# Seven products for eight in two chunk pairs of a decoder's first FFN products, and low parts made by accumulating transfers

## The chip, the cores and the metric

One core of a Trainium2 chip runs the program. The metric is device time in microseconds (us). A core has five engines that run their own instruction lists in order: PE (TensorE, matrix products into PSUM banks), DVE (VectorE), ACT (ScalarE), POOL (GpSimd) and SP (which here only issues transfers). Instructions of different engines meet through semaphores; transfers are carried by 16 DMA engines.

## The reference

Two decoder layers over 256 tokens of width 1024. Each layer is FFN, token mixing, FFN, each followed by a layer norm. All is float32. Only the FFN matters here:

```
def swiglu(x, w_in, w_out):
    gate, up = jnp.split(x @ w_in, 2, axis=-1)      # w_in 1024 x 5632
    return (jax.nn.silu(gate) * up) @ w_out         # w_out 2816 x 1024
...
for l in range(DEPTH):                              # DEPTH = 2
    x = layer_norm(alpha * x + 0.5 * swiglu(x, ffn_w_in[l, 0], ffn_w_out[l, 0]), ...)
    x = layer_norm(alpha * x + token_mixing(x, ...), ...)
    x = layer_norm(alpha * x + 0.5 * swiglu(x, ffn_w_in[l, 1], ffn_w_out[l, 1]), ...)
```

So there are four FFNs, each with a first product (`x @ w_in`) and a second one.

## The kernel before

**Split products.** PE multiplies in a float32 form of fewer bits (`F32R`). Every operand is therefore kept as a high and a low part: ACT copies a weight tile to the high part, which rounds (L78), and DVE subtracts that from the original for the low part (L79). `split` does this, mostly in tiles of 128x1024; `stage` fetches a tile from memory through SP (L86) into one of five buffers `wst`; `stream` does both for a chunk. The parts go to six pairs of buffers `wh`, `wl` and four pairs `exh`, `exl`. `mm3` makes a product out of three matmuls: high by high (L105), high by low (L106), low by high (L107).

**First product.** The 5632 columns are cut into 11 chunks of 512 (256 gate, 256 up). A chunk has four staged tiles (8 blocks of 128 rows of the weight, two to a tile), and takes 8 blocks x 2 token tiles t x 3 = 48 matmuls of 128x512 into two PSUM banks `ph`. Chunks 0 and 1 go together, the others (single chunks) one by one; their tiles are used in order, each by 12 matmuls. Behind a chunk `act` makes `g` = silu(gate) * up with ACT (`sg`, L250) and DVE (L252). `emit_T` turns g on PE (four transposes into `ptg`, L270) and splits it; for the chunks in `FAST` it also makes sums of g's quarters (`su`) and splits them. For a single chunk it is called for the chunk before, in front of the chunk's third tile.

**Second product.** Five of the 11 chunks (`FAST`) already use seven products of quarters for eight (`fast`), with the differences of weight quarters in tiles `ts`; the others are plain.

**Order.** The engine lists are made by a scheduler of the framework when the program is built; a tile of a pool waits until its buffer's last user is done. The layer norm's gain and bias (`gb`, 1 MB) are loaded by SP while the first product runs (`load_gb`).

Of the kernel before, what the change touches and what calls it, by code (L numbers as in the profile page):

```python
# [8 lines left out]
F32 = mybir.dt.float32  # L9
# [3 lines left out]
OP = mybir.AluOpType  # L13
# [12 lines left out]
NEG = -1e30  # L26

FAST = (0, 2, 4, 6, 7)
ALPHA = float((2 * DEPTH) ** 0.25)


# [20 lines left out]
def trunk(ctx: ExitStack, tc: tile.TileContext, a: dict):  # L52
# [13 lines left out]

        return wpool.tile([P, 1024], dt, tag="ex" + side, name="ex" + side, bufs=4)

    def split(src, n, cut, more=False):

        if more:
            h, l = extra("h", F32R), extra("l", F32R)
        else:
            h = wpool.tile([P, 1024], F32R, tag="wh", name="wh", bufs=SPLIT_BUFS)
            l = wpool.tile([P, 1024], F32R, tag="wl", name="wl", bufs=SPLIT_BUFS)
        for i in range(0, n, cut):
            c = slice(i, min(i + cut, n))
            nc.scalar.activation(h[:, c], src[:, c], AF.Copy)  # L78
            nc.vector.tensor_tensor(out=l[:, c], in0=src[:, c], in1=h[:, c].bitcast(F32), op=OP.subtract)  # L79
        return h, l  # L80

    def stage(src, n, cut=1024):
# [3 lines left out]
            nc.sync.dma_start(out=t[:, c], in_=src[:, c])  # L86
        return t

    def stream(src, kcs, n, cut=1024, more=False):


        out = []
        per = 1024 // n
        for k0 in range(0, kcs, per):
            m = min(per, kcs - k0)
            st = stage(src[:, k0 * n:(k0 + m) * n], m * n, cut)
            h, l = split(st[:, :m * n], m * n, min(cut, m * n), more)
# [148 lines left out]
    def ffn(l, i, first):  # L246
        with tc.tile_pool(name="fpool", bufs=1, reuse_waits="tile") as fp:
            def act(t, ps):
                sg = fp.tile([P, 256], F32, tag="sg", name="sg", bufs=3)
                nc.scalar.activation(sg, ps[:, :256], AF.Silu)  # L250
                g = fp.tile([P, 256], F32, tag="g", name="g", bufs=3)
                nc.vector.tensor_tensor(out=g, in0=sg, in1=ps[:, 256:], op=OP.mult)  # L252
                return g

# [7 lines left out]
            def emit_T(c, gs, pt=None):  # L262

                if pt is None:
                    pt = at.tile([P, 4, P], F32, tag="sc", name="ptg", bufs=2)

                at_ = ((1, 0), (2, 3)) if c in FAST else ((0, 1), (2, 3))
                for t in range(2):
                    for k in range(2):
                        nc.tensor.transpose(pt[:, at_[k][t]], gs[t][:, k * P:(k + 1) * P], ident)  # L270
                if c not in FAST:
                    h, l = parts(pt, f"g{c}")
                    gT[c] = {(k, t): (h[:, at_[k][t]], l[:, at_[k][t]]) for k in range(2) for t in range(2)}
                    return

                a10 = fp.tile([P, P], F32, tag="a10", name="a10", bufs=2)
                nc.scalar.activation(a10, pt[:, 0], AF.Copy)
                su = fp.tile([P, 4, P], F32, tag="su", name="su", bufs=2)
# [8 lines left out]
                gT[c].update({f"s{j + 1}": (sh[:, j], sl[:, j]) for j in range(4)})  # L287

            gT = {}
            pend = None  # L290
            w = {}
            for cs in ((0, 1), *((c,) for c in range(2, NCH))):
                pss = {}
                if first and cs == (0, 1):
                    warm_up()
                    w = {0: [], 1: []}
                    for k in range(0, KC, 2):
                        for c in cs:
                            w[c] += first_blocks(a["ffin"][l, i, c], k, c == 0, c == 1)
                    load_ident()  # L300
                else:
                    for c in cs:
                        w[c] = stream(a["ffin"][l, i, c], KC, 512, 512 if c == 0 else 1024,
                                      c == (0 if i == 1 else 1))
# [8 lines left out]
                if first and cs == (4,):  # L313
                    load_consts()
                    init_consts()
                for c, t, k in order:
                    if len(cs) == 1 and (t, k) == (0, 4):

                        emit_T(*pend)
                        pend = None  # L320
                    if k == 0:
                        pss[c, t] = mm.tile([P, 512], F32, tag="mm", name="ph")
                    mm3(pss[c, t], xs(t, k), w[c][k], k == 0, k == KC - 1)
                for c in cs:
                    if pend is not None:
                        emit_T(*pend)
                    pend = (c, [act(t, pss[c, t]) for t in range(2)])
                    w.pop(c)
            gb = load_gb(l, 2 * i)


# [13 lines left out]
            def fast(c):  # L345
                b0, b1 = (stage(src[:, k * 1024:(k + 1) * 1024], 1024) for k in (2 * c, 2 * c + 1))
                lo, hi = slice(0, 512), slice(512, 1024)
                u = fp.tile([P, 1024], F32, tag="ts", name="ts", bufs=2)
                v = fp.tile([P, 1024], F32, tag="ts", name="ts", bufs=2)
                tt = nc.vector.tensor_tensor  # L350

                w00 = split(b0[:, lo], 512, 512, True)
                tt(out=u[:, lo], in0=b0[:, hi], in1=b0[:, lo], op=OP.subtract)
                tt(out=u[:, hi], in0=b1[:, hi], in1=b0[:, hi], op=OP.subtract)
                w1 = split(b1, 1024, 1024, True)
                wu = split(u, 1024, 1024, True)
                tt(out=v[:, lo], in0=b1[:, hi], in1=u[:, lo], op=OP.subtract)
                tt(out=v[:, hi], in0=b1[:, lo], in1=v[:, lo], op=OP.subtract)
                wv = split(v, 1024, 1024, True)
                for n, x, w, cols in (("p1", "a00", w00, lo), ("p2", "a01", w1, lo), ("p5", "s1", wu, lo),  # L360
                                      ("p7", "s3", wu, hi), ("p6", "s2", wv, lo), ("p3", "s4", w1, hi),
                                      ("p4", "a11", wv, hi)):
# [35 lines left out]
            for c in range(NCH - tail // 2):  # L398
# [5 lines left out]
                            for h in range(2):  # L404
                                down(t, h, k)
                if c == 0:
                    emit_T(*pend, ptl)
            last = l == DEPTH - 1 and i == 1
            for t in range(2):
                for h in range(2):  # L410
# [596 lines left out]
```

## Time and profile before

| | us |
|---|---|
| median of 3 runs (1036.57 to 1037.86) | 1037.13 |
| the profiled execution's own time | 1037.3 |
| its span, first to last instruction | 1035.3 |
| PE busy | 1018.1 |
| DVE busy | 784.8 |
| ACT busy | 551.0 |
| POOL busy | 23.3 |

Time lies 2.0 us above the span in the profiled execution. Busy is time in which an engine had at least one instruction under way; PE's is modelled, and an engine can be busy at less than its best rate.

### The profile page before, as it was taken

The page shows a single profiled execution, that of the slowest core. Times are in us where ns is not written, and L with a number is a line of the kernel's source. Part 1 is how long each engine was busy: PE and PEld are TensorE (multiplying, and loading weights), DVE is VectorE, ACT ScalarE, POOL GpSimd, SP SyncE. Part 2 cuts the span into 40 slices and gives each one's busy share as a digit, 9 for nine tenths or more (in the row PEclk, how much of TensorE's full clock was granted, in tenths as well). Part 3 has the DMA queues.
Part 4 walks back from the last instruction along what each step waited for, and adds up shares of the span by engine and source line. Part 5 has one row for each costly group of instructions (what it writes and reads, how often), then busy time and mean ns, then how long its engine had stood idle before and what let it go on. Part 6 is the DMA issues. An engine that isn't in the chain of part 4 may idle for free.

```text
span 1035.3 us, 14159 instructions
## 1 busy us (share of the span) xinstructions
PE 1018.1 (98%) x5166; PEld 830.0 (80%) x5166; DVE 784.8 (76%) x1313; ACT 551.0 (53%) x916; POOL 23.3 (2%) x35
## 2 busy tenths in 40 slices
PE   9999999999999999999999999999999999999997
PEld 6888878878877888888878888888888778888785
DVE  6765978975989566687986668898679885657877
ACT  7554546435785445553644456544358744446451
POOL 0000000100000000000000000002000000000000
PEclk9999999999999999999999999999999999999998
DMA  9866646753463466674585656559515544666641
GB/s 341 295 204 185 214 148 191 263 189 114 133 230 85 165 189 182 174 232 143 171 283 163 184 183 207 178 156 326 185 34 176 187 136 152 185 190 189 197 150 41
DMA packets 59541, 190.22 MB, mean 184 GB/s; under 512 B 7120, under 2 KB 8784, under 8 KB 58704
## 3 DMA queue, kind: packets, MB, share of 16 engines
q1 hardware_dynamic: 59184, 189.07, 57.8%
q8 instruction: 40, 0.66, 0.3%
q10 hardware_dynamic: 288, 0.26, 0.1%
q14 instruction: 29, 0.24, 0.1%
HBM read 188.26 MB, written 1.05 MB: 183 GB/s over the span
## 4 chain that ended last, share of the span: by engine, by line
PE 73%; DVE 13%; DMA 7%; ACT 4%; issue 2%; DVEq 0%; ACTq 0%; SPq 0%
PE ph L107 12%; PE ph L106 12%; PE ph L105 12%; DMA wst<-in_ffout 5%; DVE wl L79 4%; PE acc L105 4%; PE acc L107 4%; PE acc L106 4%; DVE exl L79 2%; PE pj L107 2%; PE pj L105 2%; PE pj L106 2%; ACT wh L78 2%; PE ov L581 2%; PE pt L569 2%
## 5 line engine op out<-in xcount | busy, mean ns | idle before, releaser
L79 DVE TENSOR_TENSOR wl<-wst,wh 128x1024 fp32r<-128x1024 f32 (+3 forms) x276 | 304.6, 1107 | 147.5 <-ACT wh L78 144.9
L78 ACT ACTIVATE wh<-wst 128x1024 fp32r<-128x1024 f32 (+3 forms) x276 | 264.9, 968 | 233.8 <-PE ph L107 110.8
L105 PE MATMUL ph<-wh,xh 128*128 128x512 f32 x640 | 252.8, 395 | 0.3 <-ACT xh L239 0.3
L107 PE MATMUL ph<-wh,xl 128*128 128x512 f32 x640 | 250.2, 391 | 0.0
L106 PE MATMUL ph<-wl,xh 128*128 128x512 f32 x640 | 250.0, 391 | 0.0
L105 PEld LDWEIGHTS ph<-wh,xh 128*128 128x128 f32 x640 | 120.2, 188 | 25.1 <-ACT wh L154 0.7
L107 PEld LDWEIGHTS ph<-wh,xl 128*128 128x128 f32 x640 | 120.1, 188 | 25.2
L106 PEld LDWEIGHTS ph<-wl,xh 128*128 128x128 f32 x640 | 120.3, 188 | 24.5 <-DVE wl L155 0.3
L78 ACT ACTIVATE exh<-wst 128x512 fp32r<-128x512 f32 (+1 forms) x76 | 63.1, 858 | 65.9 <-PE p L107 54.3
L79 DVE TENSOR_TENSOR exl<-wst,exh 128x512 fp32r<-128x512 f32 (+1 forms) x76 | 72.1, 969 | 28.2 <-ACT exh L78 27.5
L105 PE MATMUL pj<-wh,xh 128*128 128x384 f32 (+3 forms) x224 | 78.2, 349 | 0.3
L107 PE MATMUL pj<-wh,xl 128*128 128x384 f32 (+3 forms) x224 | 77.9, 348 | 0.0
L106 PE MATMUL pj<-wl,xh 128*128 128x384 f32 (+3 forms) x224 | 77.1, 344 | 0.0
L250 ACT ACTIVATE sg<-ph 128x256 f32<-128x256 f32 x88 | 33.5, 384 | 67.1 <-PE ph L107 63.5
L252 DVE TENSOR_TENSOR g<-sg,ph 128x256 f32<-128x256 f32 x88 | 35.3, 416 | 30.0 <-ACT sg L250 29.1
L79 DVE TENSOR_TENSOR exl<-ts,exh 128x1024 fp32r<-128x1024 f32 x40 | 47.5, 1221 | 1.8 <-ACT exh L78 0.5
L105 PEld LDWEIGHTS pj<-wh,xh 128*128 128x128 f32 x224 | 42.3, 189 | 3.1 <-ACT nqS L824 0.7
L106 PEld LDWEIGHTS pj<-wl,xh 128*128 128x128 f32 x224 | 42.4, 189 | 1.8
L107 PEld LDWEIGHTS pj<-wh,xl 128*128 128x128 f32 x224 | 42.3, 189 | 1.8
L78 ACT ACTIVATE exh<-ts 128x1024 fp32r<-128x1024 f32 x40 | 40.7, 1055 | 5.8 <-PE acc L107 3.8
L218 POOL TENSOR_TENSOR mv<-mv,mhalf 128x1 f32<-128x1 f32 x12 | 11.2, 931 | 900.6 <-DVE mv L217 900.6
L548 DVE TENSOR_REDUCE nm<-sc 128x2 f32<-128x512 f32 (+2 forms) x36 | 23.0, 642 | 10.7 <-PE sc L544 10.4
(367 smaller groups left out, 1659.6 us busy)
## 6 DMA issues: line engine op xcount, KB each, us to landing
wst<-in_ffin SPq DMA_DIRECT2D x156, 512.0 KB, 4.4
wst<-in_ffout SPq DMA_DIRECT2D x88, 512.0 KB, 4.0
wst<-in_ffin SPq DMA_DIRECT2D x40, 256.0 KB, 4.0
exh<-in_w SPq DMA_DIRECT2D x16, 512.0 KB, 6.4
wst<-in_w_out SPq DMA_DIRECT2D x16, 512.0 KB, 4.7
gb<-in_lngb SPq DMA_DIRECT2D x6, 1024.0 KB, 7.2
wst<-in_w_b SPq DMA_DIRECT2D x16, 256.0 KB, 4.4
wst<-in_w_nq SPq DMA_DIRECT2D x8, 384.0 KB, 4.4
```

What stands on the lines that cost most here:

```text
L78: nc.scalar.activation(h[:, c], src[:, c], AF.Copy)
L79: nc.vector.tensor_tensor(out=l[:, c], in0=src[:, c], in1=h[:, c].bitcast(F32), op=OP.subtract)
L105: nc.tensor.matmul(out, lhsT=xh, rhs=wh, start=start, stop=False)
L106: nc.tensor.matmul(out, lhsT=xh, rhs=wl, start=False, stop=False)
L107: nc.tensor.matmul(out, lhsT=xl, rhs=wh, start=False, stop=stop)
L218: nc.gpsimd.tensor_tensor(out=mv[:, 3:4], in0=mv[:, 2:3], in1=mhalf[:, 0:1], op=OP.pow)
L250: nc.scalar.activation(sg, ps[:, :256], AF.Silu)
L252: nc.vector.tensor_tensor(out=g, in0=sg, in1=ps[:, 256:], op=OP.mult)
L548: nc.vector.tensor_reduce(out=nm[:, :n], in_=sv, axis=AX.X, op=OP.max, negate=True)
L569: nc.tensor.transpose(pt[:, b * P:(b + 1) * P], pr[:, b * P:(b + 1) * P], ident)
L581: order(nc.tensor.matmul(out[g * 64:(g + 1) * 64], lhsT=v, rhs=p_, start=i == 0, stop=i == n - 1, skip_group_check=True))
```

## The change

**Pairs in the first product.** With `PAIRS = (3, 7)`, chunks 3 and 4, and chunks 7 and 8, are made together by `fast_pair`. The two token tiles, two halves of the depth and two chunks give a product of 2x2 by 2x2 quarters, and Winograd's form makes it out of seven products. A pair's blocks are staged in two halves (j) of four tiles: b00 and b01 of the upper depth for the two chunks, b10 and b11 of the lower. In each half DVE makes four sums in place, and seven tiles are split (four of them into `ex` buffers). PE takes the products in the order p1, p5, p7, p3, p6, p2, p4, six matmuls for each half. Seven banks hold them; one ACT copy and seven DVE sums (`u1` to `u4`) join them, and `act` reads the u. Once per FFN `pair_operands` makes four combinations of the x quarters (`r` in two `wst` buffers, `sh` in the buffer of `gb`, and `sl`).

**Low parts by transfers.** For the last tile of each single chunk (2, 5, 6, 9, 10; `by_dma`) DVE no longer makes the low part. ACT writes minus the high part (a copy with scale -1), and a transfer issued by POOL adds the staged tile to it.

**Buffers.** `g` has four buffers for three, `a10` and `su` one for two, and the second product's differences (`ts`) are made in place in the staged tiles, behind the splits that read these.

```diff
+PAIRS = (3, 7)
...
     def split(src, n, cut, more=False, by_dma=False):
...
             nc.scalar.activation(h[:, c], src[:, c], AF.Copy)
+            if by_dma:
+                nc.scalar.activation(l[:, c], src[:, c], AF.Copy, scale=-1.0)
+                nc.gpsimd.dma_start(out=l[:, c], in_=src[:, c], accum_op=OP.add)
+            else:
+                nc.vector.tensor_tensor(out=l[:, c], in0=src[:, c], in1=h[:, c].bitcast(F32), op=OP.subtract)
...
+            def pair_operands():
...
+                    tt(out=r[t], in0=xTh[t].bitcast(F32).rearrange("p k s -> p (k s)"),
+                       in1=xTl[t].bitcast(F32).rearrange("p k s -> p (k s)"), op=OP.add)
+                tt(out=r[1][:, hi], in0=r[1][:, lo], in1=r[1][:, hi], op=OP.add)
+                tt(out=r[1][:, lo], in0=r[0][:, lo], in1=r[1][:, lo], op=OP.subtract)
+                tt(out=r[0][:, lo], in0=r[1][:, hi], in1=r[0][:, lo], op=OP.subtract)
+                tt(out=r[0][:, hi], in0=r[0][:, hi], in1=r[0][:, lo], op=OP.subtract)
...
+                sh = xpool.tile([P, 2, D], F32R, tag="gb", name="sh")
+                sl = fp.tile([P, 2, D], F32R, tag="sl", name="sl")
+                for t in range(2):
+                    nc.scalar.activation(sh[:, t], r[t], AF.Copy)
+                    nc.vector.tensor_tensor(out=sl[:, t], in0=r[t], in1=sh[:, t].bitcast(F32), op=OP.subtract)
...
+            def fast_pair(c, x, between):
...
+                for j in range(2):
+                    b00, b10, b01, b11 = (
+                        stage(a["ffin"][l, i, c + h][:, (4 * r + 2 * j) * 512:(4 * r + 2 * j + 2) * 512], 1024)
+                        for h in range(2) for r in range(2))
...
+                    take("p1", b00, True)
+                    tt(out=b00, in0=b01, in1=b00, op=OP.subtract)
+                    tt(out=b01, in0=b11, in1=b01, op=OP.subtract)
+                    take("p5", b00, False)
+                    take("p7", b01, True)
+                    take("p3", b11, False)
+                    tt(out=b11, in0=b11, in1=b00, op=OP.subtract)
+                    take("p6", b11, True)
+                    take("p2", b10, False)
+                    tt(out=b10, in0=b10, in1=b11, op=OP.subtract)
+                    take("p4", b10, True)
+                    for n, y in (("p1", "a00"), ("p5", "s1"), ("p7", "s3"), ("p3", "s4"), ("p6", "s2"), ("p2", "a01"),
+                                 ("p4", "a11")):
+                        for k in range(2):
+                            cols = slice(k * 512, (k + 1) * 512)
+                            mm3(pr[n], (x[y][0][:, 2 * j + k], x[y][1][:, 2 * j + k]), (w[n][0][:, cols], w[n][1][:, cols]),
+                                j == 0 and k == 0, j == 1 and k == 1)
+                    if j == 0:
+                        between()
...
+                nc.scalar.activation(u1, pr["p1"], AF.Copy)
+                tt(out=u2, in0=u1, in1=pr["p6"], op=OP.add)
+                tt(out=u3, in0=u2, in1=pr["p7"], op=OP.add)
...
             for cs in ((0, 1), *((c,) for c in range(2, NCH))):
                 pss = {}
+                if cs[0] - 1 in PAIRS:
+                    continue
...
+                if cs[0] in PAIRS:
+                    pend = fast_pair(cs[0], x_pair, emit_pend)
+                    continue
...
+                if len(cs) == 2:
+                    x_pair = pair_operands()
...
             def fast(c):
...
-                u = fp.tile([P, 1024], F32, tag="ts", name="ts", bufs=2)
-                v = fp.tile([P, 1024], F32, tag="ts", name="ts", bufs=2)
...
-                tt(out=u[:, lo], in0=b0[:, hi], in1=b0[:, lo], op=OP.subtract)
-                tt(out=u[:, hi], in0=b1[:, hi], in1=b0[:, hi], op=OP.subtract)
+                tt(out=b0[:, lo], in0=b0[:, hi], in1=b0[:, lo], op=OP.subtract)
+                tt(out=b0[:, hi], in0=b1[:, hi], in1=b0[:, hi], op=OP.subtract)
```

**DVE, at the end of chunks 3 and 4 of the first layer's second FFN.** Before, these rows stood there (`wl` are low parts of weight tiles, `su` and `g..l` parts of the turned g):

```order
L252 TENSOR_TENSOR g<-sg,ph 128x256 x2
L79 TENSOR_TENSOR wl<-wst,wh 128x1024 x3
L259 TENSOR_TENSOR g3l<-ptg,g3h 128x512
L79 TENSOR_TENSOR wl<-wst,wh 128x1024
L252 TENSOR_TENSOR g<-sg,ph 128x256 x2
L79 TENSOR_TENSOR wl<-wst,wh 128x1024 x3
```

Now DVE has there, from the first of the seven sums (p_3750 is p6) to the second tile of chunk 5:

```order
L362 TENSOR_TENSOR u_3937<-u_3936,p_3750 128x512
L86 TENSOR_TENSOR wl<-wst,wh 128x1024
L86 TENSOR_TENSOR exl<-wst,exh 128x1024
L363 TENSOR_TENSOR u_3938<-u_3937,p_3746 128x512
L367 TENSOR_TENSOR u_3936<-u_3936,p_3747 128x512
L364 TENSOR_TENSOR u_3939<-u_3938,p_3749 128x512
L365 TENSOR_TENSOR u_3937<-u_3937,p_3749 128x512
L368 TENSOR_TENSOR u_3938<-u_3938,p_3748 128x512
L366 TENSOR_TENSOR u_3937<-u_3937,p_3751 128x512
L259 TENSOR_TENSOR g<-sg,u_3936 128x256
L259 TENSOR_TENSOR g<-sg,u_3938 128x256
L86 TENSOR_TENSOR wl<-wst,wh 128x1024
```

The first `wl` is chunk 5's first tile, `exl` the low part for p4, the pair's last, and the last `wl` chunk 5's second tile, which now stands behind six sums and two g.

**ACT, behind the same pair.** Before, around the high part of g3 (`g3h`), `wh` being high parts of weight tiles:

```order
L258 ACTIVATE s2h<-su 128x512
L250 ACTIVATE sg<-ph 128x256 x2
L78 ACTIVATE wh<-wst 128x1024 x3
L258 ACTIVATE g3h<-ptg 128x512
L78 ACTIVATE wh<-wst 128x1024
L250 ACTIVATE sg<-ph 128x256 x2
```

Now:

```order
L257 ACTIVATE sg<-u_3938 128x256
L81 ACTIVATE wh<-wst 128x1024
L257 ACTIVATE sg<-u_3937 128x256
L257 ACTIVATE sg<-u_3939 128x256
L265 ACTIVATE g3h<-ptg 128x512
L83 ACTIVATE wl<-wst 128x1024
L284 ACTIVATE a_4029<-ptg 128x128
L81 ACTIVATE wh<-wst 128x1024 x2
```

The copy with scale -1 for chunk 5's last tile (L83, `wl`) stands behind `g3h`, which waits for chunk 3's transposes, and these PE makes in chunk 5 in front of its third tile.

**SP, in the same FFN.** Before, and then now, from the mixing's last weights on:

```order
L86 DMA wst<-in_w_out 128x1024 x8
L86 DMA wst<-in_ffin 128x512 x8
L86 DMA wst<-in_ffin 128x1024 x11
L203 DMA gb<-in_lngb 128x2048
L86 DMA wst<-in_ffin 128x1024 x29
```

```order
L93 DMA wst<-in_w_out 128x1024 x8
L93 DMA wst<-in_ffin 128x512 x8
L93 DMA wst<-in_ffin 128x1024 x35
L210 DMA gb<-in_lngb 128x2048
L93 DMA wst<-in_ffin 128x1024 x5
```

`gb` has moved from the middle of the first product to a place in front of its last five tiles (chunk 9's last and chunk 10's four); its buffer now holds `sh` until the second pair's p6 is done.

## Rows read from the trace of the kernel before

**Rows 1.** The page's head: span, then busy time of each engine.

```profile
span 1035.3 us, 14159 instructions
...
PE 1018.1 (98%) x5166; PEld 830.0 (80%) x5166; DVE 784.8 (76%) x1313; ACT 551.0 (53%) x916; POOL 23.3 (2%) x35
```

**Rows 2.** Windows: stretch, busy us of each engine, clock, DMA share, GB/s.

```profile
337.00:461.50 124.50, 124.50 (x572) 102.72 (x571) 81.42 (x116) 62.60 (x89) 0.93 (x1) 1.00 0.61 186
461.50:515.00 53.50, 53.41 (x240) 43.33 (x238) 46.12 (x61) 27.46 (x34) 0.93 (x1) 1.00 0.55 173
519.70:642.80 123.10, 122.31 (x561) 100.61 (x560) 86.42 (x120) 62.54 (x88) 0.92 (x1) 1.00 0.67 209
```

**Rows 3.** Waits by engine and releaser: total us, times, longest.

```profile
DVE wl L79 <- ACT wh L78: 144.9, 124, 3.1
ACT wh L78 <- PE ph L107: 110.8, 76, 2.0
```

**Rows 4.** Timeline of PE, second FFN's first product: start us, duration, line.

```profile
331.53 0.39 PE L105 MATMUL ph<-exh,xh 128*128 128x512 f32 x1
...
331.76 0.39 PE L106 MATMUL ph<-exl,xh 128*128 128x512 f32 x1
...
331.99 0.39 PE L107 MATMUL ph<-exh,xl 128*128 128x512 f32 x1
```

**Rows 5.** Timeline of PE around four transposes in the first FFN.

```profile
112.94 0.40 PE L107 MATMUL ph<-wh,xl 128*128 128x512 f32 x1
113.18 0.60 PE L270 MATMUL ptg<-ident,g 128*128 128x128 f32 x4
113.53 0.48 PE L105 MATMUL ph<-wh,xh 128*128 128x512 f32 x1
113.85 0.40 PE L106 MATMUL ph<-wl,xh 128*128 128x512 f32 x1
```

**Rows 6.** Timeline of DVE in the first FFN, instructions back to back.

```profile
104.29 0.28 DVE L280 TENSOR_TENSOR su<-a,ptg 128x128 f32<-128x128 f32 x1
104.49 0.28 DVE L281 TENSOR_TENSOR su<-ptg,a 128x128 f32<-128x128 f32 x1
...
107.49 0.55 DVE L259 TENSOR_TENSOR g7l<-ptg,g7h 128x384 fp32r<-128x384 f32 x1
107.95 0.68 DVE L259 TENSOR_TENSOR s7l<-su,s7h 128x512 fp32r<-128x512 f32 x1
108.55 0.41 DVE L252 TENSOR_TENSOR g<-sg,ph 128x256 f32<-128x256 f32 x1
...
112.67 1.22 DVE L79 TENSOR_TENSOR wl<-wst,wh 128x1024 fp32r<-128x1024 f32 x1
113.81 1.22 DVE L79 TENSOR_TENSOR exl<-wst,exh 128x1024 fp32r<-128x1024 f32 x1
114.94 1.22 DVE L79 TENSOR_TENSOR exl<-ts,exh 128x1024 fp32r<-128x1024 f32 x1
116.08 0.68 DVE L259 TENSOR_TENSOR g8l<-ptg,g8h 128x512 fp32r<-128x512 f32 x1
```

**Rows 7.** Timeline of DVE: the second x tile's low parts, second FFN.

```profile
340.44 1.36 DVE L240 TENSOR_TENSOR xl<-pt,xh 128x512 fp32r<-128x512 f32 x2 [0.45 <-ACT xh L239]
```

**Rows 8.** Timeline of ACT in the same first product.

```profile
383.34 1.06 ACT L78 ACTIVATE wh<-wst 128x1024 fp32r<-128x1024 f32 x1 [1.72 <-PE ph L107]
384.30 0.58 ACT L258 ACTIVATE g3h<-ptg 128x512 fp32r<-128x512 f32 x1
```

**Rows 9.** Transfers by line: count, KB each, median us from issue to landing.

```profile
wst<-in_ffin SPq DMA_DIRECT2D x156, 512.0 KB, 4.4
...
gb<-in_lngb SPq DMA_DIRECT2D x6, 1024.0 KB, 7.2
...
wuq<-in_wuq SPq DMA_DIRECT2D x2, 384.0 KB, 7.9
```

**Rows 10.** Windows at the program's end (columns as in rows 2).

```profile
1024.00:1028.00 4.00, 3.68 (x17) 2.67 (x15) 1.84 (x4) 0.00 (x0) 0.00 (x0) 1.00 0.35 131
1028.00:1030.00 2.00, 0.00 (x0) 0.00 (x0) 1.90 (x5) 0.00 (x0) 0.29 (x1) 0.91 0.00 0
1030.00:1032.00 2.00, 0.00 (x0) 0.00 (x0) 2.00 (x4) 0.00 (x0) 0.64 (x1) 0.50 0.00 0
```

More of the change, by code (lines that the diff above doesn't have):

```diff
@@ L67, in extra, with split @@
         return wpool.tile([P, 1024], dt, tag="ex" + side, name="ex" + side, bufs=4)
-    def split(src, n, cut, more=False):
+    def split(src, n, cut, more=False, by_dma=False):
         if more:
@@ L87, in stage, with stream @@
         return t
-    def stream(src, kcs, n, cut=1024, more=False):
+    def stream(src, kcs, n, cut=1024, more=False, by_dma=()):
         out = []
@@ L96, in stream @@
             st = stage(src[:, k0 * n:(k0 + m) * n], m * n, cut)
-            h, l = split(st[:, :m * n], m * n, min(cut, m * n), more)
+            h, l = split(st[:, :m * n], m * n, min(cut, m * n), more, k0 in by_dma)
             for i in range(m):
@@ L274, in emit_T @@
                     return
-                a10 = fp.tile([P, P], F32, tag="a10", name="a10", bufs=2)
+                a10 = fp.tile([P, P], F32, tag="a10", name="a10")
                 nc.scalar.activation(a10, pt[:, 0], AF.Copy)
-                su = fp.tile([P, 4, P], F32, tag="su", name="su", bufs=2)
+                su = fp.tile([P, 4, P], F32, tag="su", name="su")
                 tt = nc.vector.tensor_tensor
@@ new lines, in fast_pair, with take @@
+            def fast_pair(c, x, between):
+                pr = {}
+                for n in ("p1", "p7", "p2", "p4"):
+                    pr[n] = mm.tile([P, 512], F32, tag="mm", name=n)
+                for n, tag in (("p5", "pt"), ("p6", "ov"), ("p3", "sc")):
+                    pr[n] = at.tile([P, 512], F32, tag=tag, name=n, bufs=2 if tag == "sc" else 1)
+                tt = nc.vector.tensor_tensor
+                for j in range(2):
+                    b00, b10, b01, b11 = (
+                        stage(a["ffin"][l, i, c + h][:, (4 * r + 2 * j) * 512:(4 * r + 2 * j + 2) * 512], 1024)
+                        for h in range(2) for r in range(2))
+                    w = {}
+                    def take(n, src, more):
+                        w[n] = split(src, 1024, 1024, more)
+                    take("p1", b00, True)
[17 more added lines that the diff above has]
+                        between()
+                u1, u2, u3, u4 = (fp.tile([P, 512], F32, tag=f"u{n}", name=f"u{n}") for n in range(1, 5))
+                nc.scalar.activation(u1, pr["p1"], AF.Copy)
+                tt(out=u2, in0=u1, in1=pr["p6"], op=OP.add)
+                tt(out=u3, in0=u2, in1=pr["p7"], op=OP.add)
+                tt(out=u4, in0=u3, in1=pr["p5"], op=OP.add)
+                tt(out=u2, in0=u2, in1=pr["p5"], op=OP.add)
+                tt(out=u2, in0=u2, in1=pr["p3"], op=OP.add)
+                tt(out=u1, in0=u1, in1=pr["p2"], op=OP.add)
+                tt(out=u3, in0=u3, in1=pr["p4"], op=OP.add)
+                return [(c, [act(0, u1), act(1, u3)]), (c + 1, [act(0, u2), act(1, u4)])]
@@ L289, in ffn, with emit_pend @@
             gT = {}
-            pend = None
+            pend = []
             w = {}
+            def emit_pend():
+                while pend:
+                    emit_T(*pend.pop(0))
             for cs in ((0, 1), *((c,) for c in range(2, NCH))):
                 pss = {}
+                if cs[0] - 1 in PAIRS:
+                    continue
+                if first and cs[0] == 3:
+                    load_consts()
+                    init_consts()
+                if cs[0] in PAIRS:
+                    pend = fast_pair(cs[0], x_pair, emit_pend)
+                    continue
@@ L324, in ffn @@
                 for c in cs:
-                    if pend is not None:
-                        emit_T(*pend)
-                    pend = (c, [act(t, pss[c, t]) for t in range(2)])
+                    emit_pend()
+                    pend.append((c, [act(t, pss[c, t]) for t in range(2)]))
                     w.pop(c)
+                if len(cs) == 2:
+                    x_pair = pair_operands()
             gb = load_gb(l, 2 * i)
@@ L406, in ffn @@
                 if c == 0:
-                    emit_T(*pend, ptl)
+                    emit_T(*pend[0], ptl)
             last = l == DEPTH - 1 and i == 1
```

34 lines of the change are left out of this document (20 added, 14 removed).

## The prediction

> **What bounds it now.** I read the page's head first: PE is busy for 1018.1 of 1035.3 us, the other engines are not near that [rows 1]. Then the windows by stage: in the second FFN's first product (331.5 to 461) PE is busy in all of the time at full clock, DVE in 81.4 of 124.5 us, and the third FFN reads alike [rows 2]. The waits show DVE waiting for ACT's high parts, and ACT for PE to give back weight buffers [rows 3]: both run ahead of PE and are held by buffers. So the kernel is PE-bound, and a first product costs what its matmuls cost: one starts 0.227 us after another [rows 4], and four transposes add 0.36 (113.18 to 113.53) [rows 5].
>
> **What the change takes from PE.** A pair needs 7 x 4 x 3 = 84 matmuls for 96. Two pairs save 24 per first product, 5.4 us, 21.8 us in all. This is the most that can be won here: 1037.3 - 21.8 = 1015.5.
>
> **What it gives DVE.** Back to back, DVE starts an instruction of 1024 elements 1.135 us after the one before, of 512 after 0.60, of 384 after 0.46, of 128 after 0.20; a g takes about 0.33 [rows 6]. A pair has 14 splits and 8 differences for 8 splits, and 7 sums of 512: 14 x 1.135 + 7 x 0.60 = 20.1 us more. `pair_operands` adds 4 x 1.135 + 4 x 0.60 = 6.9. Five transfers take away 5 x 1.135 = 5.7. A first product gains 2 x 20.1 + 6.9 - 5.7 = 41.4 us of DVE work, on 81.4 [rows 2]: 122.8, where PE will need 119.1 (124.5 - 5.4). So DVE becomes the bound, and any time in which it can't work is lost. ACT has room: 62.6 busy [rows 2], plus 12 copies of 0.96 for the pairs, five for the transfers and a few small ones (some 20 us).
>
> **Walk through the second FFN's first product**, counted from its first matmul (331.53 [rows 4]). PE: chunks 0 and 1 take 96 x 0.227 = 21.8, chunk 2 10.9, with two turns (0.36 each) the first pair can begin at 33.4. DVE has x's last low parts at 341.8, that is 10.3 [rows 7]. From there it has `pair_operands`, three splits of chunk 2 and two g: to 20.7. Only the last of these frees the buffer for the pair's tile b11, whose load takes 4.4 [rows 9]; so b01 = b11 - b01 starts at 25.9, after the rest of `su`. From this instruction to p4's low part in the second half, DVE's list has 21 instructions of 1024 (23.8), six of 384 or 512 (3.3), `su` and two g (1.5): 28.6, and 1.1 of waiting where p4's tile is made, then copied by ACT (0.96 [rows 8]), then subtracted; with small gaps 56.1. PE has six matmuls behind it: 57.5. With nothing missing it would be done at 33.4 + 19.4 = 52.8. **PE waits 4.7**; the pair takes 24.1 us, where two chunks took 22.7.
>
> Chunk 5's first tile lasts to 60.3. Its second is split behind six sums and two g (order of DVE): the last sums need the pair's end, the g need ACT's `sg`, 61.1, and the split makes 62.3: **2.0**. In front of the third tile PE turns g3 and g4. The copy with scale -1 for the fourth tile stands behind `g3h`: turned at 65.5, copied at 66.1, scaled copy done at 67.1. Then POOL's transfer. No row shows one. Below it could cost nothing that shows (it is ready if it takes 1.5); above, the slowest kind of row of this size lands after 7.9; the nearest is the 512 KB tile, 4.4 [rows 9], which I take: 71.5. PE is done with the third tile at 68.6: **2.9**.
>
> The second pair: DVE is held in order by chunk 5's g until 74.7, has 31 us of work to p4's last low part, 106.8, and PE could be done at 85.5 + 19.4 = 104.9 but is at 108.2: **3.3**. Chunk 9's second tile behind the sums: **1.3**; its fourth, whose scaled copy stands behind the copy for `a10` and one more tile of ACT, **3.7**. `gb` (7.2 [rows 9]) now waits for p6 of this pair, at 104, with chunk 9's last tile behind it on SP: some 11 us for both, landing at about 115, where ACT comes to that tile at 116.6. I cost it at nothing, and this margin is its cover; a load 3 us longer would cost 1 to 2 per FFN, inside the transfer's bound.
>
> The sum: 17.9 us of waits less 5.4 saved is 12.5 per first product. In the first FFN the scaled copy for chunk 5 stands ahead of `g3h` in ACT's list, and its 2.9 falls away: 9.6. In all 3 x 12.5 + 9.6 = 47.1 us. The differences in place in the second product are as many instructions as before, on tiles held longer; DVE is busy 46.1 of 53.5 there [rows 2], and PE is ahead by no more than a tile. I take nothing, 2 us per FFN at most. POOL's layer-norm steps come after its transfers and wait for DVE as now. **1037.3 + 47.1 = 1084**, against a median of 1037.13, from which the profiled execution differs by 0.2.
>
> DVE's sums could be off by 5%, 1.5 us per pair, 12 in all. Bounds of the transfer over its seven places: at nothing -(3 x 2.9 + 4 x 3.7) = -23.5, at 7.9 +24.5.
>
> The Trainium skill (DMA: Bandwidth & Descriptors, section "Anatomy of one DMA — SWDGE (gpsimd) path") gives for a plain transfer of this kind 2.0 us plus bytes over 436 GB/s. That is an estimate of 3.2 us for 512 KB, by which the sum would be 7 x 1.2 = 8 us lower, 1076; no row here shows such a transfer.
>
> **Rivals.**
>
> The transfer is hidden or nearly so. For it: three of the five in every first product (chunks 2, 6, 10) have time in my walk. Against: in chunks 5 and 9 the list leaves 1.5 us or less. It gives 1061.
>
> The transfer is slow, or PE's stops lower its clock. The first gives 1109. For the second: at the end PE stops at about 1027.7, and the granted clock goes from 1.00 through 0.91 to 0.50 over the next 4 us, that is from 2.4 to 1.2 GHz [rows 10]; seven stops of 2.9 or 3.7 us stand in my sum. If half clock lasted as long as the stop that brought it, each would cost half its length more, 12 us in all: 1096. Against: these stops lie between dense stretches, the one at the end doesn't.
> On transfers the Trainium skill has a rule against the change (SBUF — State Buffer, "Summary: rules for kernel authors"): a transfer from POOL is not to be hidden under DVE work, since DVE in its faster modes keeps POOL from writing descriptors. DVE here moves 1024 elements in 1.135 us in these subtractions; the page exempts two-input operations from those modes. If it held nevertheless, a transfer would start only when DVE pauses, within a few us, which is this rival again.
>
> Faster. The mechanism: DVE's lead. Every late time above follows from DVE reaching the first pair at 25.9, held by a buffer. If it comes 4.7 us earlier, by 21.2, no wait is left in the first pair, the sums' wait falls too, and with hidden transfers DVE has only to fit: at 122.8 per first product against 124.5 now, some 1030; if the neighbouring stages carry the excess as well, 1015.5. For it: the total of DVE, 784.8 + 4 x 41.4 = 950, is still below PE's. Against: two of the three splits before 25.9 and b11's buffer can't come earlier while chunk 1 holds its weight buffers.
>
> No change: the same with waits of 5 us per first product left.
>
> **Chances.** The forecast (1070 to 1097) 0.42; hidden transfers (1045 to 1070) 0.17; slow ones or a lower clock 0.12; faster 0.21, evenly over 1013 to 1035; no change 0.08. A measurement of this kernel tells some 0.2% (2 us) from no change. So faster 0.21, same 0.08, slower 0.71. The range of 8 in 10 reaches from 1024 to 1110: it leaves out half of the faster case and part of the slow one. The likeliest case alone has 1070 to 1097.
>
> **What would show it.** PE's matmuls in `ph` and p1 to p7: 96 fewer of 128x512, each still 0.227 after another. DVE's busy time in a first product near 123 us, nearly without idle from the pair's first differences to its sums. Waits of PE for `exl` or `wl` (L86) of 4 to 5 us inside each pair and for the `wl` that POOL's transfer completes, 3 to 4 us, in chunks 5 and 9. Landing times of the transfers on POOL's queue: 4.4 is the term most likely to be off. I am wrong in kind if PE has no idle inside the pairs, that is if DVE's low parts are ready 5 us earlier than counted, or if a first product takes under 124 us.

## The result and the profile after

The changed kernel takes 1136.41 us (median of 4 runs, 1134.71 to 1139.02) against 1037.02 for the kernel before: a ratio of 1.096, 95% interval 1.0937 to 1.0982. It is 99 us slower. The forecast was 1084, and its range of 8 in 10 ended at 1110.

The head of the page of the changed kernel, as in [rows 1], with the line of the granted clock (tenths, 40 slices) and the shares of the chain that ended last:

```profile
span 1135.1 us, 14235 instructions
...
PE 1041.1 (92%) x5070; PEld 824.3 (73%) x5070; DVE 947.3 (83%) x1493; ACT 626.0 (55%) x1000; POOL 39.9 (4%) x55
...
PEclk9999999899999999989999998999999999999899
...
PE 41%; DVE 22%; DMA 16%; issue 7%; ACT 5%; SPq 0%; POOL 0%; DVEq 0%; ACTq 0%; POOLq 0%
```

PE has its 96 matmuls less (5166 to 5070) and is nevertheless busy for longer: 1041.1 us for 1018.1. It also has idle time now. To see where, I cut both traces into stages, from the first `ph` matmul of an FFN to the first that reads `g0`, from there to the last that reads a g, and on to the next stage's first matmul:

| us | before | after | more |
|---|---|---|---|
| four first products | 125.0, 125.7, 127.0, 125.7 | 151.1, 144.0, 147.5, 144.5 | 83.6 |
| four second products | 59.9, 58.9, 59.1, 58.4 | 60.6, 59.6, 59.7, 59.5 | 3.1 |
| from these to the next stage (three) | 0, 0, 0 | 8.8, 1.3, 1.6 | 11.7 |
| two mixings | 141.1, 141.2 | 141.6, 142.3 | 1.6 |

The four first products of the changed kernel as windows (columns as in [rows 2]):

```profile
5.36:156.45 151.09, 132.62 (x546) 101.68 (x545) 125.77 (x174) 89.56 (x127) 4.50 (x5) 0.95 0.68 213
367.38:511.39 144.01, 127.78 (x554) 101.38 (x552) 119.98 (x158) 78.71 (x106) 5.34 (x6) 0.96 0.58 175
572.28:719.75 147.47, 130.82 (x553) 101.81 (x553) 125.89 (x167) 79.62 (x108) 5.28 (x6) 0.97 0.61 186
923.32:1067.77 144.45, 129.48 (x553) 102.34 (x552) 119.04 (x158) 78.67 (x107) 5.32 (x6) 0.95 0.59 176
sum 587.02, PE 520.70 PEld 407.22 DVE 490.69 ACT 326.56 POOL 20.44; mean PE 130.18 PEld 101.80 DVE 122.67 ACT 81.64 POOL 5.11
```

The sum row gives 587.02 - 520.70 = 66.3 us in which PE had nothing to do. The same row of the kernel before (its four first products) has 503.39 - 502.60 = 0.8:

```profile
sum 503.39, PE 502.60 PEld 414.44 DVE 349.82 ACT 262.73 POOL 2.79; mean PE 125.65 PEld 103.61 DVE 87.45 ACT 65.68 POOL 0.70
```

DVE is busy for 122.67 us on average, for 87.45 before. The clock column is below 1.00 in all four. The waits of PE, and those of SP's queue, over the whole kernel:

```profile
PE ph L113 <- DMA wl<-wst: 34.3, 10, 4.9
PE ph L113 <- DVE wl L86: 9.3, 13, 0.8
PE pt L245 <- DVE x L234: 9.2, 3, 6.8
PE p L112 <- ACT exh L81: 6.4, 7, 1.8
...
SPq L93 <- DMA wl<-wst: 145.2, 20, 9.2
```

About half of PE's idle time is spent on the `wl` that a transfer completes. The last row is of another kind: each of the 20 transfers also stops SP's queue, 7 us on average, because the next load wants the staging buffer that the transfer still reads. A wait of this queue is no loss by itself (before, it waits 616.5 us for DVE's `wl`, with PE busy for 98% of the span); it becomes one where ACT and DVE then run out of tiles. From issue to landing (median, last column) the transfers take

```profile
wl<-wst POOLq DMA_DIRECT2D x20, 512.0 KB, 8.3
```

where I had taken 4.4 from [rows 9]. One stop, chunk 5's fourth tile in the second FFN, on PE's timeline, and then the same stretch as windows:

```profile
436.54 0.39 PE L112 MATMUL ph<-wh,xh 128*128 128x512 f32 x1
441.02 0.50 PE L113 MATMUL ph<-wl,xh 128*128 128x512 f32 x1 [4.09 <-DMA wl<-wst]
441.35 0.39 PE L114 MATMUL ph<-wh,xl 128*128 128x512 f32 x1
...
442.59 0.63 PE L112 MATMUL ph<-wh,xh 128*128 128x512 f32 x1
443.02 0.63 PE L113 MATMUL ph<-wl,xh 128*128 128x512 f32 x1
```

```profile
436.90:441.00 4.10, 0.02 (x1) 0.00 (x0) 0.56 (x1) 0.14 (x1) 0.00 (x0) 1.00 0.95 274
441.00:442.00 1.00, 0.98 (x4) 0.85 (x5) 0.00 (x0) 1.00 (x2) 0.00 (x0) 0.95 0.24 53
442.00:444.90 2.90, 2.90 (x8) 2.22 (x8) 1.53 (x3) 2.49 (x5) 0.72 (x1) 0.50 0.79 263
```

PE waits 4.1 us, does a few matmuls at full rate, and then the granted clock is 0.50 (1.2 for 2.4 GHz) for 2.9 us: matmuls start 0.43 us apart, for 0.227. Over the four first products I find 183 matmuls with long durations that start late with no wait in front of them, by 28.8 us together (46 with 4.2 us before), and 51 first ones behind a wait that start another 10.5 us late in all (0.7 before). So the 83.6 us are, by this count: 21.8 saved, 65.5 more idle, 24.6 of half clock, 9.8 of restarts, 5.5 unassigned.

### The profile page after: what moved, and what is told of

It is laid out like the page before. It is cut to its first block, busy times and chain, and to the rows that moved or that the text cites. A ratio compares the mean times of both kernels' runs of the same rounds, so it can differ in the third digit from the quotient of the medians.

```text
span 1135.1 us, 14235 instructions
## 1 busy us (share of the span) xinstructions
PE 1041.1 (92%) x5070; PEld 824.3 (73%) x5070; DVE 947.3 (83%) x1493; ACT 626.0 (55%) x1000; POOL 39.9 (4%) x55
## 4 chain that ended last, share of the span: by engine, by line
PE 41%; DVE 22%; DMA 16%; issue 7%; ACT 5%; SPq 0%; POOL 0%; DVEq 0%; ACTq 0%; POOLq 0%
DMA wst<-in_ffin 6%; DMA wl<-wst 6%; DVE wl L86 5%; DVE exl L86 5%; PE ph L113 3%; PE ph L114 3%; PE acc L112 3%; PE acc L114 3%; PE pj L114 3%; PE acc L113 3%; PE pj L112 3%; PE pj L113 3%; PE ph L112 3%; DMA wst<-in_ffout 2%; ACT wh L81 2%
## 5 line engine op out<-in xcount | busy, mean ns | idle before, releaser
L86 DVE TENSOR_TENSOR wl<-wst,wh 128x1024 fp32r<-128x1024 f32 (+3 forms) x240 | 258.3, 1086 | 31.4 <-ACT wh L81 30.9
L81 ACT ACTIVATE exh<-wst 128x1024 fp32r<-128x1024 f32 (+1 forms) x180 | 170.6, 972 | 132.8 <-DVE wst L448 43.0
L86 DVE TENSOR_TENSOR exl<-wst,exh 128x1024 fp32r<-128x1024 f32 (+1 forms) x180 | 197.3, 1114 | 38.2 <-ACT exh L81 36.8
L113 PE MATMUL ph<-wl,xh 128*128 128x512 f32 x384 | 161.6, 421 | 43.7 <-DMA wl<-wst 34.3
L112 PE MATMUL ph<-wh,xh 128*128 128x512 f32 x384 | 158.8, 416 | 4.1 <-ACT wh L81 3.8
L114 PE MATMUL ph<-wh,xl 128*128 128x512 f32 x384 | 158.5, 413 | 0.0
L113 PEld LDWEIGHTS ph<-wl,xh 128*128 128x128 f32 x384 | 76.7, 200 | 69.0 <-DMA wl<-wst 38.9
L112 PEld LDWEIGHTS ph<-wh,xh 128*128 128x128 f32 x384 | 76.2, 199 | 22.2 <-ACT wh L81 5.1
L114 PEld LDWEIGHTS ph<-wh,xl 128*128 128x128 f32 x384 | 77.2, 201 | 16.1 <-DVE xl L247 0.2
L277 PE MATMUL ptg<-ident,g 128*128 128x128 f32 x176 | 28.4, 282 | 4.2 <-DVE g L259 4.2
```

The costliest lines, as they stand in the source:

```text
L112: nc.tensor.matmul(out, lhsT=xh, rhs=wh, start=start, stop=False)
L113: nc.tensor.matmul(out, lhsT=xh, rhs=wl, start=False, stop=False)
L114: nc.tensor.matmul(out, lhsT=xl, rhs=wh, start=False, stop=stop)
```

## The experiments

Times are medians; the kernel before was at 1037.0 to 1038.3 beside them.

**Undoing the parts.** Four versions of the changed kernel. The first two:

```diff
-                                      c == (0 if i == 1 else 1), (KC - 2,) if c > 1 else ())
+                                      c == (0 if i == 1 else 1), ())
```

> The changed kernel with its 20 accumulating transfers taken back: DVE splits those tiles again. Theory A (the transfers, 8.3 us each, are most of the loss: stops of 3 to 5 us behind ten of them, the half clock after the stops, and the loads that wait until a transfer has read its buffer): 1136 - 35 of stops - some 25 for clock and late loads, about 1075. Theory B (the pairs are the loss: DVE has too much to do): DVE gets 20 x 1.135 = 23 us more work and the time stays at 1120 to 1145.

Measured: 1087.0. By this the transfers cost 49 us, net of the 23 that they spare DVE. That is nearer A, but A's place for the loss did not hold (below), and 49 us over before remain.

```diff
-PAIRS = (3, 7)
+PAIRS = ()
...
```

> The changed kernel without its pairs and their operands: nine single chunks in each first product, each with its last quarter by an accumulating transfer (36 of them). Theory A: a transfer of 8.3 us stops PE wherever it is, 1037 + 12 (second product and layer norm, as in the changed kernel) + 36 x 3 = about 1155. Theory B: with DVE and ACT ahead of PE as before the transfers are hidden, 1045 to 1055.

Measured: 1087.1, neither. No wait of PE on a transfer is left in this trace. It waits for what stands behind late loads (in the second FFN ACT, in front of the high part of g10, waits 4.6 us for a tile of the second product's weights):

```profile
PE acc L112 <- DVE g10l L266: 19.4, 4, 5.6
PE ptg L277 <- DVE g L259: 9.3, 3, 3.3
...
SPq L93 <- DMA wl<-wst: 282.5, 36, 11.4
```

Both edits at once:

> Neither pairs nor transfers: what is left of the change is the second product's differences in place, the smaller buffers a10 and su, one more g and the constants' load one chunk earlier. By the changed kernel's trace the second products cost 3 us more and the layer norm after the first FFN stops PE for 7 us more: if these belong to the differences in place, 1037 + 3 + 8.7 = about 1049; if they come from the pairs or the transfers, 1037.

Measured: 1058.9 (ratio 1.0195, 1.0176 to 1.0213). The first products are as long as before (125.7 in the second FFN). The second products take 9.9 us more, and what follows them 11.7, as in the changed kernel. So the part that I had costed at nothing costs 21 by itself. And against this run the 36 transfers of the one before it cost 1087.1 - 1058.9 = 28 us, 13 in the first products and 15 in the second ones, though DVE is busy there for only 57% of the four first products:

```profile
sum 517.88, PE 507.42 PEld 416.97 DVE 296.11 ACT 291.49 POOL 34.37; mean PE 126.86 PEld 104.24 DVE 74.03 ACT 72.87 POOL 8.59
```

The fourth has one pair:

```diff
-PAIRS = (3, 7)
+PAIRS = (3,)
```

> One pair instead of two (chunks 3 and 4), seven transfers in each first product instead of five. PE saves 10.9 us. Theory A: the 28 transfers cost about 3 us each as in the changed kernel, 1037 - 11 + 12 + 84 = about 1122. Theory B: half of the pairs' loss goes, about 1090.

Measured: 1136.6: half of the pairs with 28 transfers is as slow as two pairs with 20. More transfers took what one pair less gave, which theory B excludes and A undersizes.

**The differences in place.** The second product gets two tiles of its own again, in the bytes of `sl`, free by then (the transfers stay out in the first of these runs; the third, without pairs, has the tiles `ts` of the kernel before):

```diff
+                uv = fp.tile([P, 2, D], F32, tag="sl", name="uv")
+                u, v = uv[:, 0], uv[:, 1]
-                tt(out=b0[:, lo], in0=b0[:, hi], in1=b0[:, lo], op=OP.subtract)
+                tt(out=u[:, lo], in0=b0[:, hi], in1=b0[:, lo], op=OP.subtract)
...
```

> No transfers, two pairs, and the second product's differences in two tiles of their own again (in the bytes of the pairs' tile sl, which is free by then). If the differences in place are the 20 us of the run without pairs and transfers, 1087 - 20 = about 1067, with PE's stop at the end of the first FFN gone; by the changed kernel's own stages (3 + 11.7) 1072. Rival: the pairs bring this stop themselves, by DVE's delay: 1087.

Measured: 1073.3 (1066.8 to 1074.9). The stops behind the second products are gone.

> The changed kernel, pairs and transfers kept, with the second product's differences in tiles of their own. If the differences in place cost here what they cost without transfers (1087 - 1073 = 14): 1136 - 14 = about 1122. Rival: in the changed kernel the second product is late anyway, by chunk 10's transfer: 1131 or more.

Measured: 1123.2. The term is 13 to 14 us with pairs, 21 without.

> The run with neither pairs nor transfers (1059), its second product given two tiles of its own again; a10, su, g and the constants' load stay as changed. If the differences in place are the whole of its 20 us: 1037 to 1039. If the smaller buffers have a part: 1042 or more.

Measured: 1038.0 (ratio 0.9997, 0.9985 to 1.0009). The small buffers and the constants' load cost nothing in a kernel without pairs. What the 8.8 us behind the first FFN are shows in the changed kernel's timelines of PE, POOL and DVE there:

```profile
216.79 0.40 PE L114 MATMUL acc<-exh,g10l 128*128 128x512 f32 x1
223.96 1.97 PE L245 MATMUL pt<-ident,x 128*128 128x128 f32 x8 [6.78 <-DVE x L234]
```

```profile
214.96 0.95 POOL L569 MEMSET exl<- 128x1024 f32 x1 [71.23 <-PE acc L113]
215.96 0.56 POOL L225 TENSOR_TENSOR mv<-mv,mhalf 128x1 f32<-128x1 f32 x1
```

```profile
214.38 0.14 DVE L224 TENSOR_SCALAR mv<-mv 128x1 f32<-128x1 f32 x1
...
220.20 1.41 DVE L228 SCALAR_TENSOR_TENSOR x<-x,mv,gb 128x512 f32<-128x512 f32 x2
...
223.16 1.41 DVE L234 SCALAR_TENSOR_TENSOR x<-x,mv,gb 128x512 f32<-128x512 f32 x2
```

The framework's scheduler has put a memset of `exl` for the mixing ahead of the layer norm's power on POOL (the power starts 1.4 us after its input is there), and, which costs more, DVE's last step for the first token tile (L234), for which the power was done at 216.5, behind all of the second tile's steps. Before, and with tiles of its own, the power comes first and the first tile's step stands with its own tile. Why the scheduler decides so was not tried.

**The transfers.** First, who else could make these low parts: POOL itself.

```diff
-                nc.scalar.activation(l[:, c], src[:, c], AF.Copy, scale=-1.0)
-                nc.gpsimd.dma_start(out=l[:, c], in_=src[:, c], accum_op=OP.add)
+                nc.gpsimd.tensor_tensor(out=l[:, c], in0=src[:, c], in1=h[:, c].bitcast(F32), op=OP.subtract)
```

> The changed kernel, with the 20 low parts subtracted by POOL itself in place of the copy with scale -1 and the accumulating transfer. If the loss of the transfers is their 8.3 us until landing, it goes, and DVE keeps the 5.7 us per first product that it won: 1087 - 23 = about 1064. POOL's time for 1024 elements is not known: a memset of this size takes it 0.95 us, so some 2 to 4 us. Rival: the place of the work is the loss (the low part is begun too late for whoever makes it), then the stops stay, about 1120. Third: POOL slows DVE while it runs, 1085 to 1100.

Measured: 1093.6, the third case: 43 us better than the transfers and 7 worse than DVE alone (1087.0). The last section has why.

Fewer transfers:

```diff
-                                      c == (0 if i == 1 else 1), (KC - 2,) if c > 1 else ())
+                                      c == (0 if i == 1 else 1), (KC - 2,) if c in (2, 6, 10) else ())
```

> Transfers only in chunks 2, 6 and 10: 12 of 20 are left, those without a stop except chunk 2 of the first FFN. If the stops are the cost: 1087 + 4 - 12 x 1.135 = about 1078. Rival: every transfer costs the same 2.3 us (46 us by 20), by the loads that wait until it has read its buffer: 1087 + 28 = 1115.

Measured: 1117.5, the rival: 30 us for 12 transfers, 2.5 each, as 49 for 20. (Stops of PE on transfers: 12.6 us, where I had 4.) So theory A, that the stops are the cost, was in doubt. Two runs then took apart what a transfer does. In one, the kernel before gets 36 transfers that nobody waits for:

```diff
             nc.vector.tensor_tensor(out=l[:, c], in0=src[:, c], in1=h[:, c].bitcast(F32), op=OP.subtract)
+            if idle and idle[1]:
+                nc.gpsimd.dma_start(out=idle[0][:, c], in_=src[:, c], accum_op=OP.add)
+            elif idle:
+                nc.gpsimd.dma_start(out=idle[0][:, c], in_=src[:, c])
...
```

> The kernel before, with a transfer from POOL added to the last quarter of chunks 2 to 10, into a tile that nobody reads: plain in even chunks, accumulating in odd ones. Landing: if accumulation is what is slow, some 8 us against 3 to 5; if any transfer between tiles that POOL starts is slow, 8 for both. Time: if only those who wait for the result lose, 1037; if the held buffer delays the loads and so PE, 1042 to 1060.

Measured: 1037.3 (ratio 0.9994, 0.998 to 1.0008); landing, from the views of the accumulating and then of the plain line (minimum, median, maximum):

```profile
DMA to landing us min/median/max: 6.6/8.3/9.2
```

```profile
DMA to landing us min/median/max: 2.9/5.8/7.4
```

Moving the data costs nothing here, in a kernel whose DVE idles for a third of a first product. What a held buffer costs, this run doesn't show: 34 of the 36 transfers start when the load has landed, beside ACT's and DVE's own reading of the tile, so they hold the buffer little longer than DVE does. SP's queue waits for 21 of them, and not for long:

```profile
SPq L90 <- DMA scr<-wst: 57.8, 21, 5.8
```

The 36 transfers of the run without pairs, which start behind ACT's second copy, made it wait for 282.5 us. In the other, the transfers are begun before the chunk's other three tiles:

```diff
-        for k0 in range(0, kcs, per):
+        for k0 in sorted(range(0, kcs, per), key=lambda k: k not in by_dma):
...
```

> Pairs, transfers and own tiles, as in the run of 1123 us, but a chunk's last quarter is loaded, copied and sent off before its other three. If the transfers cost because they begin too late for PE: the stops of 3 to 5 us and the half clock behind them go, 1123 - 34 - 10 = about 1079, and down to 1050 if DVE uses all of the 23 us that it is spared. Rival, the held staging buffer delays the loads behind it: 1105 or more.

Measured: 1120.5, where the same kernel without this edit had 37.8 us of stops on transfers and took 1123.2. No wait of PE on a transfer is left; it waits for DVE and ACT instead. Theory A fell. The next run tests what was left, with transfers that only hold the staging buffer (from the run of 1073.3 us):

```diff
+            def unread(src):
+                for i, n in enumerate(("u3", "u4")):
+                    z = fp.tile([P, 512], F32, tag=n, name="z")
+                    nc.gpsimd.memset(z, 0.0)
+                    nc.gpsimd.dma_start(out=z, in_=src[:, i * 512:(i + 1) * 512], accum_op=OP.add)
...
```

> Two pairs, own tiles, all low parts by DVE (the run of 1073 us), and behind each low part where the change has a transfer two accumulating transfers of 512 columns from the staging buffer into tiles that nobody reads. If the held staging buffer is the transfers' cost: 1073 + 30 to 50 = 1105 to 1120. If it is not: 1073 to 1080.

Measured: 1118.1, 45 us more, though neither PE nor DVE waits for a transfer. SP's queue does:

```profile
SPq L95 <- DMA z<-wst: 134.5, 20, 9.1
```

Two rivals are out by this trace: DVE's low parts take 1.22 us as before, so POOL's memsets don't slow them, and the loads of 512 KB land after 4.6 us (4.5 without transfers), so they don't lack bandwidth. What grows is DVE's idle time in the four first products. The sums of the windows, first without the transfers, then with them, give 539.36 - 500.75 = 38.6 us and 572.37 - 490.33 = 82.0, that is 43 of the 45 us:

```profile
sum 539.36, PE 505.99 PEld 399.32 DVE 500.75 ACT 307.30 POOL 2.78; mean PE 126.50 PEld 99.83 DVE 125.19 ACT 76.82 POOL 0.70
```

```profile
sum 572.37, PE 520.42 PEld 404.82 DVE 490.33 ACT 300.12 POOL 55.08; mean PE 130.11 PEld 101.20 DVE 122.58 ACT 75.03 POOL 13.77
```

Their tiles are the pairs' `u3` and `u4`, for whose last reader POOL waits, so they do not start exactly when the change's transfers do.

The edit of the last two runs, on the runs of 1120.5 and of 1073.3 us:

```diff
-        t = wpool.tile([P, 1024], F32, tag="wst", name="wst", bufs=5)
+        t = wpool.tile([P, 1024], F32, tag="wst", name="wst", bufs=6)
-            l = wpool.tile([P, 1024], F32R, tag="wl", name="wl", bufs=SPLIT_BUFS)
+            l = wpool.tile([P, 1024], F32R, tag="wl", name="wl", bufs=5)
...
```

> The run of 1120 us (transfers begun first in their chunk) with six staging buffers for five and, for the space, five buffers wl for six. If the held staging buffer is the cost: at or below the 1073 of no transfers, or some 10 above it for the missing wl. If not: 1115 or more.

> The run of 1073 us with the same exchange of a wl for a staging buffer: shows what the exchange is worth without transfers. By either theory 1065 to 1085.

Measured: 1102.5 and 1065.0. A sixth staging buffer takes 18 us from the kernel with transfers and 8 from the one without: what the transfers cost falls from 47 to 38. The direction is that of the theory, its size is not: one more buffer relieves a fifth, and I had expected nearly all. The wait itself did not go: SP's queue still waits 87.0 us for transfers, for 92.9 with five buffers.

**The pairs.** With own tiles and no transfers, one pair late, one pair early, and two late ones (`PAIRS` is `(7,)`, `(3,)` and `(5, 8)`, in the run of 1073.3 us):

> One pair (chunks 7 and 8), no transfers, the second product's differences in tiles of their own. PE saves 10.9 us. DVE gets 81.4 + 20.1 + 6.9 = 108.4 us per first product, less than PE's 121.8. Theory A (a pair costs only where DVE has no lead): DVE is ahead by its buffers when the pair comes, so 1037 - 11 and up to 3 us of waits per first product: 1026 to 1038. Theory B (each pair brings its waits wherever it stands: with two pairs and own tiles 8 pairs cost 36 us, 4.5 each): 1037 + 18 = about 1055.

Measured: 1032.2, ratio 0.9941 (0.9928 to 0.9955): faster than both kernels, by 0.6% than the one before. A first product's window:

```profile
329.50:453.90 124.40, 123.60 (x565) 101.41 (x564) 104.12 (x141) 68.64 (x95) 0.93 (x1) 1.00 0.57 178
```

> The same with the pair at chunks 3 and 4. Theory A: DVE reaches the pair late, held by x and the pairs' operands (the prediction's 4.7 and 2.0 us of waits), and PE's clock falls behind the stops (some 2): 1037 - 11 + 4 x 8.7 = about 1061. Theory B: about 1055, as for the late pair.

Measured: 1051.3, lower than either: the place alone is worth 19 us.

> Two pairs at chunks 5, 6 and 8, 9, no transfers, own tiles. If DVE's total of work bounds the first product with two pairs: 1073 or more, since DVE is held by full buffers in chunks 2 to 4 and has all of both pairs to do after them. If the late arrival at the first pair is the loss: two times the late pair's gain, 1026 to 1050.

Measured: 1065.9, between the two cases and nearer to the first: 7 us below pairs at 3 and 7 and 34 above one late pair. So most of the loss with two pairs goes with DVE's total, a smaller part with the late arrival. The windows of a first product with two pairs, early (first row) and late, show DVE at work in nine tenths of it:

```profile
341.10:477.30 136.20, 127.00 (x554) 100.88 (x554) 123.32 (x162) 74.62 (x102) 0.93 (x1) 0.97 0.52 163
```

```profile
337.90:468.80 130.90, 125.50 (x555) 100.44 (x555) 119.11 (x157) 73.63 (x100) 0.93 (x1) 0.99 0.51 165
```

## Why the prediction was wrong

**Right: what PE saves, and that DVE becomes the bound.** 96 matmuls are gone. I had 41.4 us more DVE work per FFN; over the whole kernel it is (947.3 - 784.8) / 4 = 40.6. That my 122.8 for a first product meets the mean of 122.67 is luck: I added to 81.4, a window of the second FFN that leaves out its first 5.5 us, where the mean of the whole first products is 87.45. A first product gained 35.2, and the rest of the work moved into the stages behind it.

**Right: the walk through the first pair.** p4's last low part was to be ready at 56.1; it starts at 422.94 and ends with the next instruction's start, 424.08, that is 56.7 after the first matmul at 367.38. PE enters the pair at 34.6 (33.4 in the walk) and leaves it at 58.5 (57.5). POOL issues chunk 5's transfer at 432.63, that is 65.3 (67.1).

```profile
422.94 1.23 DVE L86 TENSOR_TENSOR exl<-wst,exh 128x1024 fp32r<-128x1024 f32 x1 [0.49 <-ACT exh L81]
424.08 0.68 DVE L363 TENSOR_TENSOR u<-u,p 128x512 f32<-128x512 f32 x1
...
432.63 0.86 POOL L84 DMA_DIRECT2D wl<-wst  x1 [40.73 <-ACT wl L83]
```

**Right in the sum, not in its parts: PE's waits.** I had 3 x 17.9 + 15.0 = 68.7 us; PE idles for 66.3. But 34.3 of them are waits for transfers, where I had 23.5, and so only 32 are left for the pairs and their sums, where I had 45. The near agreement of the sums is chance.

**Wrong: the transfer as a term.** "The nearest is the 512 KB tile, 4.4, which I take": the median is 8.3, above even my upper bound of 7.9. The step that failed is another: I charged a transfer only where PE waits for its result (23.5 us in all), and called three of five hidden. Taking the transfers out gives back 49. With pairs a transfer costs 2.4 to 2.5 us, net of the 1.1 that it spares DVE, whether PE waits for it (20 and 12 transfers) or not (begun earlier); one that is not read and spares DVE nothing costs 2.2. If the spared 1.1 counts in full, that is 3.6 gross, and the held buffer alone makes about two thirds of it (an estimate from these runs); the rest (ACT's second copy, later data) was not taken apart. The way is this: a transfer holds one of five staging buffers until it lands (SP's queue waits 7 us each time); SP's loads are in order, so the loads behind it come late; and DVE stands still for them (43 us more in the four first products with unread transfers). That a sixth buffer gave back only a fifth leaves open how many it would take.

The cost also depends on the kernel around it, and DVE's idle time does not settle it. The unread transfers in the kernel before cost nothing, but they hardly outlast the buffer's other readers. The 36 read ones without pairs cost 28 us, 0.8 each net, beside a DVE that idles for over 40% of a first product. With one early pair DVE is busy for 72% of the first products, and yet 1136.6 - 1051.3, less 14 to 21 for the differences in place, leaves 2.3 to 2.5 for each of 28. What sets the price between 0.8 and 2.5 was not tried. The prediction asked what the transfer delays at its end and not what it keeps occupied at its source, though it had done so for b11's buffer in the same walk.

**Wrong: the second product.** "I take nothing, 2 us per FFN at most. POOL's layer-norm steps come after its transfers and wait for DVE as now." They don't: behind the first FFN a memset stands ahead of the power, and DVE's last step for the first token tile behind the second tile's. Measured: 13.2 us (1136.4 to 1123.2); by the stages most of it lies at the ends of the second products, 8.8 behind the first.

**Wrong: no loss of clock in the forecast.** The rival had 12 us for it; half clock took 24.6. The argument against it, that the stops lie between dense stretches, does not protect: the clock fell behind stops of 4 us in the middle of them.

Together: the forecast's 47.1, less 3.2 of waits (65.5 for 68.7), and 24.6 of half clock, 9.8 of restarts, 14.8 behind the first products and 1.6 in the mixing make 94.7; with the 5.5 unassigned it is 100.2, where the spans differ by 99.8. Undone one after another, the parts are 49 (transfers), 14 (in place) and 35 (pairs), 98 in all.

**The rivals.** Slow transfers came true, but two more terms with them, and no single case reached 1136. "Faster" was not out of reach: with one pair, placed late, no transfers and the second product's own tiles, 6 us of at most 10.9 are won.

## What to carry to other kernels

A transfer out of a staging buffer is paid for by the loads that wait for this buffer: before handing work to one, count the buffers in the ring, ask by how much it outlasts the buffer's other readers, and look at what SP's queue and then DVE wait for. Here 36 such transfers cost nothing where they started with the other readers, 28 us where they started behind them, and 20 cost 49 us beside two pairs. An engine's mean idle time did not tell which it would be. Saving PE work at DVE's expense paid with one pair, late, where DVE's total stays below PE's and its buffers are full ahead of PE; the same pair placed early lost 13 us.

## What the runs showed of the hardware

**Accumulating transfers.** 512 KB between SBUF tiles, issued by POOL beside the kernel's loads, landed after 8.3 us accumulating and 5.8 plain (medians of 16 and 20 in the run with unread transfers in the kernel before). The Trainium skill (DMA: Bandwidth & Descriptors, "Anatomy of one DMA — SWDGE (gpsimd) path") leads to an estimate of 3.2 for a plain one; the fastest plain one here, at 2.9, is near it, the median is not.

**POOL and DVE shut each other out.** In the run with POOL's subtractions, POOL's instruction and DVE's in the same stretch:

```profile
30.90 2.39 POOL L83 TENSOR_TENSOR wl<-wst,wh 128x1024 fp32r<-128x1024 f32 x1 [30.07 <-DVE g L258]
...
31.02 0.29 DVE L286 TENSOR_TENSOR su<-a,ptg 128x128 f32<-128x128 f32 x1
...
31.62 2.77 DVE L85 TENSOR_TENSOR wl<-wst,wh 128x1024 fp32r<-128x1024 f32 x1
```

POOL needs 2.4 us here; over the 20 it takes up to 3.4, the longest where such a subtraction of DVE was under way first. DVE's small sum with an operand in PSUM (`ptg`) is not slowed (0.29, as in [rows 6]); its subtraction with both operands in SBUF takes 2.77 for 1.22, until 1.1 after POOL's end at 33.29. The Trainium skill (SBUF — State Buffer, "SBUF: two separate sides") has this as an exclusive lock between the two, for DVE operations with two SBUF inputs against POOL operations that read SBUF; the rows agree. The other 19 stretches agree: of the DVE instructions that start behind POOL's start, those with both operands in SBUF end 0.3 to 1.1 us after POOL's end, and those with one in PSUM keep their usual time. Against the median of the same instruction elsewhere in this trace, DVE's take 29 us longer in all. Spared were 20 x 1.135 = 23 us, and the run was 6.6 us slower than with DVE alone.
